# Output projection of a hybrid attention block as seven products of halves, with the gates in another order

## The chip, the cores and the metric

The kernel runs on one core of a Trainium2 chip. A core has a matrix engine (PE; it loads a 128 x 128 block of weights, then multiplies a moving operand into one of eight PSUM banks), a vector engine (DVE), a scalar engine (ACT), a small general engine (POOL) and an engine that only issues transfers (SP). ACT and POOL issue transfers too. All five run their own queues, each in order, and wait for each other through semaphores. The metric is the device time of one execution in microseconds (us); the kernel before takes 1464.66, the median of three runs.

## The reference

One layer over 1024 tokens of 1024 channels, in float32. Two branches work on the same normalised input, gates merge them, and the output projection, to which the change belongs, adds the result to the input:

```python
xn = rmsnorm(x, norm1_g[layer])
u = xn @ w_in[layer].astype(f32)
...
g_a = jax.nn.sigmoid(gate_sb + bg[:D_MODEL])
g_b = jax.nn.sigmoid(gate_hg + bg[D_MODEL:])
merged = g_a * (o_sb @ w_o_sb[layer].astype(f32)) + g_b * (o_hg @ w_o_hg[layer].astype(f32))
h = x.astype(f32) + merged @ w_out[layer].astype(f32)
hn = rmsnorm(h, norm2_g[layer])
a = jnp.square(jax.nn.relu(hn @ w_ff1[layer].astype(f32)))
h = h + a @ w_ff2[layer].astype(f32)
```

`o_sb` is a stick-breaking attention of 8 heads, `o_hg` a gated linear recurrence of 4 heads. A last `rmsnorm` gives the output.

## The kernel before

**Number format.** Each float32 operand of a product is split into a rounded part h (a cast on ACT, `hi_copy`, line 142) and the rest l = x - h (a subtraction on DVE, `lo_sub`, line 147); `hi_lo` does both. `three` (line 490) multiplies h·h, h·l and l·h into one PSUM bank, so a product over 128 channels is three matmuls. The gates and both halves of the MLP are already computed with seven products of halves in place of eight (Winograd's form: sums of operands are multiplied, and the results summed); the output projection is not.

**Stages.** Input norm and transposes; the attention in 64 blocks (8 heads x 8 blocks of queries, `items`), between which pieces of other projections are run; the recurrence; eight gate blocks of 128 channels (`GatePair`, driven by `gates`); the output projection (`wout_job`); the second norm (`norm2_token`) and the transposes of its result (`Quads.fill`, tile hnt, called fills here); the MLP up (`UpPair`) and down.

**Tiles.** SBUF holds 40 large tiles of 1024 columns (`slot`), 10 half ones (`half`), and two each of raw, h and l weight tiles (`wpool`). A tile becomes free when its last reader is done; a transfer that loads into one waits for that. `load` issues on SP's queue, and each load is kept behind the last one.

**Order on PE.** Matmuls belong to one of two lanes, "main" and "fill" (`open_block`); within a lane PE runs them in the order in which the program emits them. On the other engines the order comes from a planner that takes, among the instructions that are ready, the earliest in the program; `after` adds an order by hand.

**Gates.** For channel block cb, `x6`, `y5`, `x7` and `y3` are four products of the gate weights, `hg_product` two of the recurrence's output projection. `late_half` makes the merged activations of tokens 512 to 1023, `early_half` those of tokens 0 to 511. `out` (line 1365) splits the early half into h and l at once, in tiles `mgs`; the late half goes to DRAM (`md`), except for cb 6 and 7, and `late_merged` (line 1375) loads and splits it later.

**Output projection.** `wout_job(n)` covers the columns n x 512 to n x 512 + 511: for each of 8 blocks of 128 tokens, 8 channel blocks x 3 matmuls go into one bank `pw`, which DVE adds to `hres[tb]`, a tile of 128 rows of x (line 1462). `Stream.prefetch` splits the weights ahead. In the second column half each token block is followed by its norm: `norm2_token` squares on ACT, takes a power on POOL, scales on DVE, and stores `hres[tb]` to DRAM from SP (line 1434). From token block 4 on, a fill of two finished token blocks (16 transposes) follows each block, and then the first two MLP pairs begin on half of the tokens.

## Time and profile before

| | |
|---|---|
| runs | 1464.66, 1464.33, 1466.59 us |
| profiled execution | 1464.93 us, of it 1463.1 in the span from the first to the last instruction |
| granted clock of PE | 0.996 of full speed |
| attention | 59.7 to 317.5 us |
| gate blocks | 617.2 to 747.8 us |
| output projection with the first fills | 747.8 to 840.3 us |
| MLP down | 1148.3 to the end |

Times in the profile are us from the span's start, durations of a single instruction ns unless marked. In a row of a group, `out<-in` are the program's tile names without their numbers, `L1462` is a line of the kernel, `x16` the count; then come busy time, mean of one, and the idle time of the engine before them with what ended it. PE busy counts overlapping matmuls once. The durations of matmuls overlap (each is 389 ns long and the next starts earlier), so their cost is read from the spacing in the chain of waits, not from the duration.

### The profile page before, as it was taken

Reading aid. Unit: us, or ns where it says so; the run is one execution under the profiler, and the core shown is the slowest. Engines: PE = TensorE matmul, PEld = TensorE weight load, DVE = VectorE, ACT = ScalarE, POOL = GpSimd, SP = SyncE. Lnnn points to the kernel's source line nnn. Section 1 sums busy time; section 2 is a strip of 40 time slices with the busy share of each in tenths; the row PEclk is TensorE's granted clock in tenths of the full one; section 3 lists DMA queues with packets and bytes.
Section 4 is the critical chain, followed back from the end, with each engine's and each line's share of the span. In section 5 each row is a group of like instructions: output and inputs, shape, how many; then the busy total and the mean of one; then the engine's idle time right before and its main releaser. Section 6 shows DMA issues by size and latency. Waiting matters only on the chain.

```text
span 1463.1 us, 19989 instructions
## 1 busy us (share of the span) xinstructions
PE 1446.2 (99%) x7538; PEld 1231.7 (84%) x7538; DVE 1071.7 (73%) x1545; ACT 655.9 (45%) x1162; POOL 103.5 (7%) x282
## 2 busy tenths in 40 slices
PE   8999999999999999999999999999999999999997
PEld 8889988988898888888888888888888888888885
DVE  6699798798747778877664598666666757768764
ACT  7566666552322334523341574444444533524343
POOL 3020010000000012100000100000000000000041
PEclk9999999999999999999999999999999999999999
DMA  6123022002203249645363133444445974776824
GB/s 205 37 62 73 8 59 65 16 15 62 88 19 101 73 134 252 234 152 159 113 232 108 78 102 129 158 157 148 156 158 185 350 267 175 260 276 249 279 99 161
DMA packets 150248, 206.85 MB, mean 141 GB/s; under 512 B 24668, under 2 KB 92296, under 8 KB 150152
## 3 DMA queue, kind: packets, MB, share of 16 engines
q1 hardware_dynamic: 141464, 182.76, 36.9%
q0 software_dynamic: 5088, 16.26, 4.2%
q10 hardware_dynamic: 3600, 6.56, 1.2%
q8 instruction: 59, 0.97, 0.3%
q14 instruction: 37, 0.30, 0.1%
HBM read 147.35 MB, written 49.81 MB: 135 GB/s over the span
## 4 chain that ended last, share of the span: by engine, by line
PE 91%; DVE 4%; DMA 2%; POOL 1%; issue 1%; ACT 1%; SPq 0%; POOLq 0%; ACTq 0%; DVEq 0%
PE pm L121 18%; PE pX L121 9%; PE pjqk L121 6%; PE pw L121 6%; PE pY L121 6%; PE pW L121 6%; PE pjv L121 3%; PE pjq L121 3%; PE pys L121 3%; PE pyh L121 3%; PE gY L121 3%; PE gX L121 3%; PE pji L121 3%; PE pjf L121 3%; PE pjg L121 3%; PE po L121 3%
## 5 line engine op out<-in xcount | busy, mean ns | idle before, releaser
L142 ACT CAST whid<-w 128x1024 fp32r<-128x1024 f32 x31 | 32.6, 1053 | 153.5 <-PE pm L121 89.2
L679 DVE TENSOR_TENSOR_SCAN rm<-rm,bits 128x511 f32<-128x511 f32 (+7 forms) x72 | 87.3, 1219 | 15.2 <-ACT rm L657 13.5
L121 PE MATMUL pm<-wlod,sh 128*128 128x512 f32 x248 | 96.6, 390 | 0.8 <-DVE wlod L147 0.8
L121 PE MATMUL pm<-whid,sl 128*128 128x512 f32 x248 | 96.5, 389 | 0.0
L121 PE MATMUL pm<-whid,sh 128*128 128x512 f32 x248 | 96.5, 389 | 0.0
L147 DVE TENSOR_TENSOR wlod<-w,whid 128x1024 fp32r<-128x1024 f32 x31 | 37.9, 1222 | 58.1 <-ACT whid L142 58.1
L121 PE MATMUL pm<-th,sh 128*128 128x512 f32 x200 | 77.8, 389 | 0.0
L121 PE MATMUL pm<-tl,sh 128*128 128x512 f32 x200 | 77.8, 389 | 0.0
L121 PE MATMUL pm<-th,sl 128*128 128x512 f32 x200 | 77.8, 389 | 0.0
L147 DVE TENSOR_TENSOR sl<-sa,sh 128x1024 fp32r<-128x1024 f32 x56 | 68.2, 1218 | 0.1
L142 ACT CAST wTh<-pw 128x512 fp32r<-128x512 f32 (+3 forms) x96 | 44.5, 487 | 46.3 <-PE pw L124 39.7
L142 ACT CAST sh<-sa 128x1024 fp32r<-128x1024 f32 x56 | 57.2, 1046 | 10.7 <-DMA sa<-ad 10.7
L147 DVE TENSOR_TENSOR wTl<-pw,wTh 128x512 fp32r<-128x512 f32 (+3 forms) x96 | 50.7, 547 | 9.2 <-ACT wTh L142 5.6
L121 PEld LDWEIGHTS pm<-wlod,sh 128*128 128x128 f32 x248 | 46.6, 188 | 11.0 <-DVE wlod L147 1.2
L121 PEld LDWEIGHTS pm<-whid,sh 128*128 128x128 f32 x248 | 46.5, 188 | 9.7
L121 PEld LDWEIGHTS pm<-whid,sl 128*128 128x128 f32 x248 | 46.5, 188 | 9.6
L155 DVE TENSOR_TENSOR bt<-bt,rm 128x511 f32<-128x511 f32 (+7 forms) x72 | 48.9, 686 | 5.0 <-ACT wf0h L142 0.5
L657 ACT ACTIVATE rm<-z 128x511 f32<-128x511 f32 (+6 forms) x96 | 47.5, 501 | 6.5 <-DVE bt L155 3.3
L121 PE MATMUL pX<-sqh,t1h 128*128 128x512 f32 x128 | 49.9, 390 | 0.0
L121 PE MATMUL pX<-sql,t1h 128*128 128x512 f32 x128 | 49.8, 389 | 0.0
L121 PE MATMUL pX<-sqh,t1l 128*128 128x512 f32 x128 | 49.8, 389 | 0.0
L660 ACT ACTIVATE bt<-z 128x127 f32<-128x127 f32 (+4 forms) x96 | 47.6, 504 | 0.4 <-PE po L121 0.4
(895 smaller groups left out, 4495.3 us busy)
## 6 DMA issues: line engine op xcount, KB each, us to landing
w<-in_w_ff_dram SPq DMA_DIRECT2D x72, 512.0 KB, 4.8
sa<-ad SPq DMA_DIRECT2D x56, 512.0 KB, 7.1
ad<-a SPq DMA_DIRECT2D x32, 256.0 KB, 2.9
ad<-s SPq DMA_DIRECT2D x16, 512.0 KB, 5.6
x<-in_x_dram SPq DMA_DIRECT2D x8, 512.0 KB, 9.6
xnl<-xnh POOLq DMA_DIRECT2D x8, 512.0 KB, 11.3
pr<-pd SPq DMA_DIRECT2D x8, 512.0 KB, 6.1
yr<-yd SPq DMA_DIRECT2D x8, 512.0 KB, 7.7
```

What stands on the lines that cost most here:

```text
L121: return pe(nc.tensor.matmul(*a, **k))
L142: in_turn("act", nc.scalar.copy(dst, src))
L147: nc.vector.tensor_tensor(out=dst, in0=src, in1=hi.bitcast(F32), op=ALU.subtract),
L155: return nc.vector.tensor_tensor(out=out, in0=a, in1=b, op=ALU.mult)
L657: nc.scalar.activation(rm[:, s0 + c0 - 1 : s0 + m - 1], z[:, c0:m], AF.Sigmoid, scale=-0.125)
L660: nc.scalar.activation(bt[:, s0 : s0 + e], z[:, :e], AF.Sigmoid, scale=0.125)
L679: sc = nc.vector.tensor_tensor_scan(out=rr, data0=rr, data1=bits[:, 1024 - nk + a : 1024 - nk + b][:, ::-1], initial=rm[:, b : b + 1] if i ...
```

## The change

The projection is cut into halves of tokens, of channels and of columns, 512 each, and computed by seven products of 512 x 512 x 512.

- The sums of weight blocks that these need (`tw`) are built in DRAM during the attention: four plain copies and four accumulating transfers on POOL's queue, one after every sixth attention block (`out_weight_sums`).
- The sums of merged activations are built on DVE in `out`, and go to DRAM in six forms (`fd`). For that channel blocks cb and cb + 4 must be known together, so `gates` takes the blocks in the order 0, 4, 1, 5, 2, 6, 3, 7. One half form of the last block is split from SBUF, the others are loaded again.
- `out_operands` loads and splits weight forms and merged forms; `out_product` is one block of 128 tokens of one product: 4 channel blocks x 3 matmuls.
- Products in order: 11 (bank W), then 2, 3 and a on top of each other in four banks X, then 1 (Y), b (V) and 4 (Z). `out_start` runs the first four, `out_rest` Y and V, `out_last` Z. After Y the second half of the tokens is finished, so `rows` renames token blocks: `hres[0]` to `hres[3]` are tokens 512 to 1023.
- x is loaded into `hres[4]` to `hres[7]`, and added to `hres[0]` to `hres[3]` by accumulating transfers from POOL once ACT has written W there.
- Norms of token blocks 0 to 3 follow Y, the first two fills stand in V, the norms of 4 to 7 follow Z, with the third fill behind the third Z block. `hres` is stored by POOL in place of SP. The first MLP pair's weights go to large tiles.

```diff
-    md = [dram(f"md{kp}", [P, 2, 512]) for kp in range(KT // 2)]
+    tws = dram("tw", [512, 4, 512])
+    tw = {i: tws[:, i - 1, :] for i in range(1, 5)}
+    fd = {m: [dram(f"fd{m}{kp}", [P, 2, 512]) for kp in range(2)] for m in "1234ab"}
+    def out_block(i, j):
+        return W_OUT[i * 512 : (i + 1) * 512, j * 512 : (j + 1) * 512]
+    def out_weight_sums():
+        b11, b12, b21, b22 = (out_block(i, j) for i in range(2) for j in range(2))
+        for i, src in ((1, b11), (3, b12), (2, b22), (4, b21)):
+            after(nc.gpsimd.dma_start(tw[i], src), lastsel[0])
+            yield
+        for i, src in ((1, b12), (3, b22), (2, tw[1]), (4, tw[2])):
+            after(nc.gpsimd.dma_start(tw[i], src, accum_op=ALU.add), lastsel[0])
+            yield
...
-            if i == 1 and kp < 3:
-                nc.gpsimd.dma_start(md[kp][:, j, :], y)
+            if self.cb < 4:
+                if i == 0:
+                    if j == 0:
+                        mgs.make(0, kp)
+                    hi_lo(*(t[:, j * 512 : (j + 1) * 512] for t in mgs.t[0, kp]), y)
                 return
-            if (i, kp) not in mgs.t:
-                mgs.make(i, kp)
-            h, l = (t[:, j * 512 : (j + 1) * 512] for t in mgs.t[i, kp])
-            hi_lo(h, l, y)
-    def late_merged(kp):
-        r = slot(f"mr{kp}")
-        load(r.rearrange("p (k t) -> p k t", k=2), md[kp])
-        hi_lo(*mgs.make(1, kp), r)
+            def put(m, t):
+                nc.gpsimd.dma_start(fd[m][kp - 2][:, j, :], t)
+            a, b = gp[self.cb - 4].y, self.y
+            a11, a21, a12, a22 = (t[:, c : c + 512] for t in (a, b) for c in (0, 512))
+            if i == 1:
+                s1 = half(f"fs1{self.cb}")
+                sub(s1, a21, a22)
+                put("a", a22)
+                sub(a21, a11, a21)
+                put("3", a21)
+                sub(a11, s1, a11)
+                if self.cb < 7:
+                    put("2", a11)
+                else:
+                    out_operands(m=["2"], last=a11)
+                put("1", s1)
+            else:
+                put("b", a12)
+                s4 = self.p[:, 512:1024]
+                add(s4, a12, a11)
+                put("4", s4)
...
+    gates_in = [gp[4 * i + j] for j in range(4) for i in range(2)]
     def gates():
-        for cb in range(KT):
-            v = gp[cb]
-            n = gp[cb + 1] if cb + 1 < KT else None
+        for v, n, m in zip(gates_in, gates_in[1:] + [None], gates_in[2:] + [None] * 2):
             v.x6()
             v.y5()
             if n:
                 n.split(v.u2_sum)
                 n.load_sums()
-                if cb + 2 < KT:
-                    gp[cb + 2].load()
+                if m:
+                    m.load()
             else:
-                wout_units[0][0].split()
+                out_form["11"].split()
+                out_operands(["2"])
...
-        nc.sync.dma_start(hd[tb], hres[tb])
-    def wout_job(n):
...
+        nc.gpsimd.dma_start(hd[tb], hres[tb])
+    def out_unit(name, src):
+        pieces = [src[i * 256 : (i + 1) * 256, :].rearrange("(k p) c -> p k c", p=P) for i in range(2)]
+        return Unit(f"wout{name}", [[(0, 512, t)] for t in pieces], wide=True)
+    out_form = {"11": out_unit("11", out_block(0, 0))}
+    merged = {}
+    def out_operands(w=(), m=(), last=None):
+        for n in w:
+            src = tw[int(n)] if len(n) == 1 else out_block(int(n[0]) - 1, int(n[1]) - 1)
+            out_form[n] = out_unit(n, src)
+            out_form[n].split()
+        for n in m:
+            merged[n] = []
+            for kp in range(2):
+                r = slot(f"m{n}r{kp}")
+                h, l = slot(f"m{n}h{kp}", F32R), slot(f"m{n}l{kp}", F32R)
+                merged[n].append((h, l))
+                if kp == 0 or last is None:
+                    load(r.rearrange("p (k t) -> p k t", k=2), fd[n][kp])
+                    hi_lo(h, l, r)
+                else:
+                    load(r[:, 0:512], fd[n][kp][:, 0, :])
+                    hi_lo(h[:, 0:512], l[:, 0:512], r[:, 0:512])
+                    hi_lo(h[:, 512:1024], l[:, 512:1024], last)
+    def out_product(ps, a, w, tb, start):
+        open_block("fill")
+        for k in range(4):
+            c = k % 2 * 512
+            sh, sl = (t[:, c + tb * P : c + (tb + 1) * P] for t in merged[a][k // 2])
+            wh, wl = (t[:, c : c + 512] for t in out_form[w].hl[k // 2])
+            three(ps, sh, sl, wh, wl, start and k == 0, k == 3, True)
+    def rows(tb):
+        return slice((tb + 4) % NT * P, ((tb + 4) % NT + 1) * P)
+    left, right = slice(0, 512), slice(512, 1024)
+    oW, oX, oY = {}, {}, {}
+    def turn_dve(ins):
+        in_turn("dve", ins)
+    def out_start():
+        merged["11"] = [mgs.t[0, kp] for kp in range(2)]
+        for tb in range(NT):
+            hres.append(slot(f"h{tb}"))
+        for tb in range(4):
+            load(hres[4 + tb], X[rows(4 + tb), :])
+        out_operands(["3"], ["3"])
+        for tb in range(4):
+            W = bank(f"pwW{tb}")
+            out_product(W, "11", "11", tb, True)
+            nc.scalar.activation(hres[tb][:, right], W, AF.Identity, scale=-1.0)
+            nc.scalar.copy(hres[tb][:, left], W)
+            h = hres[4 + tb]
+            turn_dve(sub(h[:, right], h[:, right], W))
+            turn_dve(add(h[:, left], h[:, left], W))
+            if tb == 1:
+                out_operands(["4"])
+        for tb in range(4):
+            oX[tb] = bank(f"pwX{tb}")
+            out_product(oX[tb], "2", "2", tb, True)
+            h = hres[4 + tb][:, right]
+            turn_dve(sub(h, h, oX[tb]))
+            nc.gpsimd.dma_start(hres[tb], X[rows(tb), :], accum_op=ALU.add)
+            if tb == 0:
+                out_operands(m=["a"])
+            if tb == 2:
+                out_operands(["1"])
+        for tb in range(4):
+            out_product(oX[tb], "3", "3", tb, False)
+            h = hres[tb][:, right]
+            turn_dve(sub(h, h, oX[tb]))
+            if tb == 0:
+                out_operands(m=["1"])
+            if tb == 1:
+                out_operands(["21"])
+            if tb > 1:
+                pairs[tb - 2].load()
+        for tb in range(4):
+            out_product(oX[tb], "a", "4", tb, False)
+            h = hres[tb][:, left]
+            turn_dve(add(h, h, oX[tb]))
+            if tb == 1:
+                out_operands(m=["b"])
+            if tb == 2:
+                out_operands(["22"])
+            if tb > 1:
+                pairs[tb - 2].split()
+    def out_rest(tb):
+        if tb < 4:
+            oY[tb] = bank(f"pwY{tb}")
+            out_product(oY[tb], "1", "1", tb, True)
+            for h in (hres[tb][:, right], hres[4 + tb][:, right]):
+                turn_dve(add(h, h, oY[tb]))
+        else:
+            W = bank(f"pwV{tb}")
+            out_product(W, "b", "21", tb - 4, True)
+            h = hres[tb][:, left]
+            turn_dve(add(h, h, W))
+    def out_last(tb):
+        Z = bank(f"pwZ{tb}")
+        out_product(Z, "4", "22", tb, True)
+        h = hres[4 + tb][:, right]
+        turn_dve(add(h, h, Z))
...
-                if self.j in (1, 2):
+                if self.j < 3:
...
-            q.dma_start(OUT[tb * P : (tb + 1) * P, cs], y[:, cs])
+            q.dma_start(OUT[rows(tb), cs], y[:, cs])
...
+    wsums = out_weight_sums()
...
             scores(*items[i + 2])
+        if i % 6 == 5:
+            next(wsums, None)
...
-    gp[1].load()
+    gates_in[1].load()
     gates()
...
-    st2.finish(j_wout - 2)
-    st2.advance(7, j_wout - 1)
-    first[0].load()
-    first[0].split()
-    first[0].sums()
-    st2.finish(j_wout - 1)
-    first[1].load()
+    out_start()
     g2b[0] = slot("g2b")
     load(g2b[0], norm2_g[0].partition_broadcast(P))
-    for tb in range(NT):
-        st2.advance(1, j_wout)
-        if tb == 1:
-            first[1].split()
-            first[1].sums()
+    sides = {}
+    for tb in range(4):
+        out_rest(tb)
+        sides[tb] = norm2_token(tb)
+        next(sides[tb])
+        if tb > 0:
+            next(sides[tb - 1], None)
+    for tb in range(4):
+        out_rest(4 + tb)
+        if tb == 0:
+            next(sides[3], None)
+        if tb < 2:
+            first[tb].sums()
+        if tb == 0:
+            out_operands(m=["4"])
+        if tb > 1:
+            hn.fill(tb - 2, hsrc, "hn")
+        if tb == 3:
+            hn.sums(0, 1)
+    for tb in range(4, NT):
+        out_last(tb - 4)
         if tb == NT - 1:
             for u in first:
                 last_evac[0] = after(u.sum_hi(1), last_evac[0])
@@ -1946,20 +2068,16 @@
         next(side)
         if tb == NT - 1:
             hn.sums(2, 1, then=False)
-        if tb in (4, 5, 6):
-            hn.fill(tb - 4, hsrc, "hn")
-        if tb == 5:
-            hn.sums(0, 1)
+        if tb == 6:
+            hn.fill(2, hsrc, "hn")
         for _ in side:
             pass
-        if tb == 6:
-            hn.sums(1, 1)
-    st2.finish(j_wout)
     pairs[2].load()
     first[1].w1(0, 256)
     first[0].w2(0, 256)
     first[0].sum_lo(1)
     first[1].w2(0, 256, range(2))
+    hn.sums(1, 1)
     hn.fill(3, hsrc, "hn")
     first[1].w2(0, 256, range(2, 4))
     for u in first:
```

More of the change, by code (lines that the diff above doesn't have):

```diff
@@ L1401 @@
     hres = []
-    st2 = Stream(eager=True)
-    wout_units = []
     hn = Quads()
@@ L1433, in norm2_token @@
         hd[tb] = dram(f"hd{tb}", [P, D])
-        nc.sync.dma_start(hd[tb], hres[tb])
-    def wout_job(n):
-        cs = slice(n * 512, (n + 1) * 512)
-        units = [
-            Unit(
-                f"wout{n}{i}",
-                [[(0, 512, W_OUT[i * 256 : (i + 1) * 256, cs].rearrange("(k p) c -> p k c", p=P))]],
-                wide=True,
-            )
-            for i in range(4)
-        ]
-        wout_units.append(units)
-        def body():
-            for tb in range(NT):
-                if n == 0:
-                    if tb < 3:
-                        late_merged(tb)
-                    hres.append(slot(f"h{tb}"))
-                    load(hres[tb], X[tb * P : (tb + 1) * P, :])
-                    if tb in AHEAD_AT:
-                        st2.prefetch()
-                ps = bank(f"pw{n}_{tb}")
-                for kt in range(KT):
-                    sh, sl = mgs.stat(kt, tb)
-                    wh, wl = (w[:, kt % 2 * 512 : (kt % 2 + 1) * 512] for w in units[kt // 2].hl[0])
-                    three(ps, sh, sl, wh, wl, kt == 0, kt == KT - 1)
-                nc.vector.tensor_tensor(
-                    out=hres[tb][:, cs], in0=hres[tb][:, cs], in1=ps, op=ALU.add
-                )
-                yield
-        return st2.add(units, body)
@@ L1469 @@
-    AHEAD_AT = (2, 4, 6)
-    for n in range(2):
-        j_wout = wout_job(n)
+        nc.gpsimd.dma_start(hd[tb], hres[tb])
[22 more added lines that the diff above has]
+                    hi_lo(h[:, 512:1024], l[:, 512:1024], last)
```

1 line of the change is left out of this document (removed).

## The prediction

> **What bounds the kernel now.** I read first the busy shares of the page, then the chain of waits that ended last, then a table of windows by stage.
>
> ```profile
> span 1463.1 us, 19989 instructions
> PE 1446.2 (99%) x7538; PEld 1231.7 (84%) x7538; DVE 1071.7 (73%) x1545; ACT 655.9 (45%) x1162; POOL 103.5 (7%) x282
> ...
> 747.95 70.72 PE pw L121 x312
> 818.67 1.75 PE hnt L124 x16
> 820.41 5.46 PE pw L121 x24
> 825.88 1.75 PE hnt L124 x16
> 827.62 5.46 PE pw L121 x24
> 833.08 1.75 PE hnt L124 x16
> 834.83 5.46 PE pw L121 x24
> ...
> 846.18 1.75 PE hnt L124 x14
> 847.93 6.47 PE pW L121 x54
> 854.40 5.47 PE pX L121 x24
> ```
>
> Columns of the chain are start, length, what. PE is the bound, and in the output projection (pw, 312 + 3 x 24 = 384 matmuls) it is the whole chain: 70.72 / 312 = 0.2267 us a matmul, 24 for one block of 128 tokens in 5.44 us. Four bursts of 16 transposes (hnt, the "fills", 1.75 us each) stand between and behind the blocks. So a matmul removed here is time removed, as long as nothing else becomes late. What could is in the windows (us; then busy time of PE, PEld, DVE, ACT, POOL with instruction counts, clock, DMA share, GB/s):
>
> ```profile
> 617.20:747.80 130.60, 130.60 (x578) 108.12 (x577) 93.05 (x132) 43.56 (x59) 3.37 (x7) 1.00 0.45 145
> 747.80:834.80 87.00, 87.00 (x410) 72.78 (x409) 41.72 (x57) 26.65 (x53) 4.48 (x12) 1.00 0.41 151
> 834.80:870.00 35.20, 34.55 (x207) 30.66 (x206) 32.57 (x55) 25.33 (x49) 2.72 (x5) 1.00 0.33 105
> 747.80:893.00 145.20, 144.55 (x716) 122.50 (x715) 94.99 (x140) 65.67 (x122) 7.20 (x17) 1.00 0.37 132
> 59.70:317.50 257.80, 256.54 (x1625) 229.18 (x1623) 227.64 (x324) 166.22 (x383) 28.69 (x152) 1.00 0.17 42
> ```
>
> The gates (617.2 to 747.8) and the projection up to its last block (834.8) have PE without a gap and DVE at 71% and 48%. From 834.8 on, where the MLP is entered, DVE is at 32.57 / 35.20 = 92.5%, and there PE has its only gap, 0.65 us. The last line is the attention.
>
> **The change part by part.**
>
> **1. Fewer matmuls.** Seven products of 512 x 512 x 512 are 7 x 4 token blocks x 4 k x 3 = 336 matmuls in place of 384, of the same shape. 48 x 0.2267 = **-10.9 us**. One block of one product takes 12 x 0.2267 = 2.72 us, the whole stage 76.2 us in place of 87.0. Nothing here is uncertain but a slower matmul, for which there is no reason.
>
> **2. Weight sums in the attention.** Eight transfers of 1 MB, DRAM to DRAM, four of them accumulating, go on POOL's queue, one every sixth of 64 blocks. Blocks take (317.2 - 59.9) / 64 = 4.0 us, so one every 24 us:
>
> ```profile
> L124 PE MATMUL pw<-ident,bt x288: 270/272/300, 59.9 to 317.2; 128*128 128x128 f32 x144
> ...
> L1175 POOL DMA_DIRECT2D xnl<-xnh x8 | 7.2, 944 | 29.4 <-PE pjg L121 26.9 <-PE pgq L121 2.4
> ...
> DMA to landing us min/median/max: 4.7/11.3/15.3
> L590 POOL DMA_DIRECT2D QH<-QH x16 | 8.7, 544 | 106.5 <-ACT QH L142 85.0 <-ACT wTh L142 12.8 <-DVE bt L155 8.7
> ```
>
> The nearest row is the accumulating xnl<-xnh: 512 KB, 0.94 us of POOL, 4.7 to 15.3 us to land. POOL is busy 28.69 of 257.8 us and the DMA share is 0.17, so both have room: 8 x 0.94 = 8 us of POOL, hidden by its idle time. Behind a transfer on POOL stand the memsets of bt and wT and the copies of QH and QL; score blocks run two blocks, some 8 us, ahead. The last sum (tw4 += tw2) must wait on POOL for tw2 += tw1 issued 24 us before. At twice the longest row, 30.6 us, POOL stands 6.6 us, still under the 8. Value 0; bounds 0 and +4 (if half of that lead is gone). The Trainium skill, page "DMA: Bandwidth & Descriptors", section "Anatomy of one DMA — SWDGE (gpsimd) path", prices such a transfer at about 2.0 us plus bytes over 436 GB/s, an estimate of 4.4 us for 1 MB. By it POOL never waits and the sum is the same 0; the trace does not bear it out for accumulating ones, 11.3 us median where it gives 3.2.
>
> **3. Gates in pairs (0, 4, 1, 5, ...).** The products and the loads of each block are the same; only their order changes, so SP's queue gets as many. Blocks 4 to 7 lose one split (a cast and a subtract of 512 columns) and gain three subtracts and an add; the two late splits of 6 and 7 go as well. POOL gets 24 stores for 6.
>
> ```profile
> L147 DVE TENSOR_TENSOR msl<-yr,msh 128x512 fp32r<-128x512 f32 x10 | 6.9, 693 | 6.4 <-ACT msh L142 6.3
> L1368 POOL DMA_DIRECT2D md<-yr x6 | 3.2, 540 | 92.1 <-DVE yr L1072 92.1
> ```
>
> DVE: (16 - 6) x 0.69 = +6.9 us into 130.6 - 93.05 = 37.6 us of idle; POOL 18 x 0.54 = 9.7 us into an idle engine. Operands of a block are made one block (16.3 us) ahead, which hides it: 0, and +6.9 if that cover were gone. The first product needs only blocks 0 to 3, done 16 us earlier; block 7's last half, which the projection waited closely for, is now needed last.
>
> **4. Loads of the projection.** Sixteen product blocks (the first 43.5 us) come with four loads of x (128 rows each), five weight forms, four merged forms, two pairs of MLP weights and four accumulations of x: about 15 MB.
>
> ```profile
> 748.00:760.00 12.00, 12.00 (x54) 9.95 (x53) 7.56 (x10) 5.25 (x7) 0.00 (x0) 1.00 1.00 372
> ```
>
> At the 372 GB/s of this full window that is 42 us. But only 10 MB (28 us) are needed inside the 43.5 us; the forms of the last two products and the MLP weights have 10 to 30 us more. The x accumulations (512 KB each) can start when ACT has written W, at about 4, 7, 10 and 12 us, and are needed from 24 us on by a DVE sum, by PE (whose fourth product waits for that sum) from 33 to 41. Two at a time, as the xnl rows ran, they land by 30 us: 0. One after another at 11.3 us the fourth lands at 49: +8. I take 0: the rows overlapped. SP issues its loads in order and each waits for free tiles: of the 40 large tiles I count 36 to 40 in use through these 43.5 us, so a form is loaded about one product (10.9 us) ahead and no more.
>
> **5. DVE's load.** The projection's sums:
>
> ```profile
> L1462 DVE TENSOR_TENSOR h<-h,pw 128x512 f32<-128x512 f32 x16 | 11.0, 686 | 22.5 <-PE pw L121 22.3 <-DMA h<-in_x_dram 0.2
> L147 DVE TENSOR_TENSOR msl<-mr,msh 128x1024 fp32r<-128x1024 f32 x3 | 3.7, 1226 | 2.5 <-ACT msh L142 2.5
> L142 ACT CAST msh<-mr 128x1024 fp32r<-128x1024 f32 x3 | 3.2, 1053 | 4.8 <-DMA mr<-md 4.8
> ```
>
> Sums of h: W 8, the three X 4 each, Y 8, V 4, Z 4, in all 36 for 16: 20 x 0.69 = +13.7. Splits of 1024 columns behind 747.8: five weight and five merged forms of two pieces and one form's two, 22, for 4 + 3 = 7: 15 x 1.23 = +18.4. Two short splits less: -1.4. That is +30.7, so from 747.8 to 893 DVE needs 125.7 us in 145.2 - 10.9 = 134.3: **93.6%**, against 65% before. ACT gets 15 x 1.05 and 8 copies of W, 21 us, and stays at 65%. At the best share that a stretch with this work shows (19.11 of 20.00 us, below) 125.7 us fit in 131.5: no loss. At the 92.5% of 834.8 to 870 they take 135.9: 1.6 us too long. At the 86% of the stage before the gates (66.45 of 77.00) 146: 11.9.
>
> ```profile
> 540.00:617.00 77.00, 76.84 (x425) 64.30 (x424) 66.45 (x98) 34.71 (x65) 16.35 (x23) 1.00 0.74 220
> 850.00:870.00 20.00, 20.00 (x107) 17.29 (x106) 19.11 (x24) 14.81 (x20) 0.00 (x0) 1.00 0.23 73
> ```
>
> Much of it is made ahead, but what is late at the end is paid in full: the first form for the MLP (sql below) is finished as pX starts at 854.40. I take **+2.0**, bounds 0 and +12.
>
> ```profile
> 852.95 2.36 DVE L147 TENSOR_TENSOR sql<-hnq,sqh 128x1024 fp32r<-128x1024 f32 x2 [0.79 <-ACT sqh L142]
> ```
>
> **6. The norm's chain against shorter blocks.** A token block's way from its last matmul to its transposes is sum, square, power, scaling:
>
> ```profile
> 818.71 0.69 DVE L1462 TENSOR_TENSOR h<-h,pw 128x512 f32<-128x512 f32 x1 [1.34 <-PE pw L121]
> 819.49 1.06 ACT L1418 ACTIVATE hn<-h 128x1024 f32<-128x1024 f32 x1 [4.35 <-DVE h L1462]
> 821.00 0.55 POOL L233 TENSOR_TENSOR n_y<-n_ss,expo 128x1 f32<-128x1 f32 x1
> 821.59 1.28 DVE L1429 SCALAR_TENSOR_TENSOR hn<-h,n_y,g2b 128x1024 f32<-128x1024 f32 x1 [2.19 <-POOL n_y L233]
> ```
>
> It ends at 822.87, 4.2 us after the block did (818.67). Blocks took 5.44 us, so it was covered. In the new order the third fill, which takes blocks 4 and 5, is emitted right behind the third Z block, 2.72 us after block 5's own; PE keeps that order, so it stands 4.2 - 2.72 = **+1.5** (bounds 0 and +3, when DVE is busy with the first two fills' splits). The fourth fill's gap, 0.65 us now, follows one Z block closer on the third; ACT has that fill's copies, two casts of 1.1 us and the last squares to do in between: **+0.4**, bounds -0.65 and +2. The stores of h move from SP to POOL: 8 x 0.54 us there, issued as soon as the sum is done, while the square runs: 0, up to 0.5.
>
> **Sum:** -10.9 + 1.5 + 2.0 + 0.4 = -7.0. The profiled execution took 1464.93 us around its span of 1463.1, 0.3 above the median of 1464.66. 1464.93 - 7.0 = 1457.9; from the median 1457.7. I say **1458**.
>
> **The rivals.**
>
> **All hidden (1454 to 1455.5).** Terms 5 and 6 vanish: 1464.7 - 10.9 = 1453.8. For it: 48% DVE use before 834.8. Against it: the order of block 5 and the third fill is fixed, so about 1 us stays.
>
> **DVE eats most of it (1461 to 1467).** DVE waits for loads that land late and keeps 87 to 90% where 93.6 are wanted: 125.7 / 0.89 = 141.2, 6.9 us over, and the 1.5 of term 6 with it: 1453.8 + 8.4 = 1462. For it: in the gates, with the same kinds of operations, it idles 29%, on ACT and PE. Against it: those idle stretches were not under load.
>
> **DVE becomes the bound (slower, about 1470).** It is one queue in order; a split whose load is late holds up the sums behind it, PE then waits for a free bank. This decides from a share of 125.7 / 145.2 = 86.6%: below that the stage is longer than before. At 83%, between the 86% before the gates and their 71%, it takes 151.4, 6.2 us more than 145.2: 1470.9. Against it: it needs idle time in a queue whose work is mostly ready 10 us ahead.
>
> **The sums by transfer stop the attention.** If an accumulation of 1 MB takes over 24 + 8 = 32 us, POOL holds the memsets and PE stands for what is over. To be worse than no change it must take over 39; the row scales to 30.6 at most.
>
> **How the numbers follow.** A measurement here can tell about 0.2% (2.9 us) from no change: faster is below 1461.7, slower above 1467.6. Chances: forecast (1455.5 to 1461) 0.52, all hidden 0.14, DVE eats most 0.20 (a quarter of it still under 1461.7), DVE bound 0.11, attention stopped 0.03. Faster 0.71, same 0.15, slower 0.14. The range goes from all hidden, 1454, through the second rival to 1467; outside are the two slow cases and a little at the low end.
>
> **What would show it.** Right: 336 matmuls between the gates and the first MLP product, a gap of 1 to 3 us before the third fill's block 5 transposes (released by DVE hn), DVE above 90% from the projection to the MLP's first pairs, attention and gates as long as before. Wrong: PE gaps in the attention with POOL as releaser (part 2); gaps before products released by a load or a split (4, 5); PE waiting in the MLP's entry for sql by more than 3 us; or no gap at the third fill.

## The result and the profile after

The changed kernel takes 1470.49 us (median of 6 runs, 1469.50 to 1471.36), the kernel before 1464.87 beside it: a ratio of 1.0036, 95% interval 1.0026 to 1.0046. It is 5.6 us slower where 7 us less were forecast, and above the range. From the page of the changed kernel:

```profile
span 1469.2 us, 20065 instructions
...
PE 1441.4 (98%) x7490; PEld 1227.8 (84%) x7490; DVE 1105.7 (75%) x1591; ACT 671.9 (46%) x1180; POOL 132.0 (9%) x319
...
q0 software_dynamic: 11376, 35.40, 9.3%
```

PE has its 48 matmuls less (7490 for 7538) and less busy time, yet the span grew by 6.1 us. The table of windows says where (columns as in the prediction); first three stretches of the attention, the gates, the projection up to the first MLP product pX, three parts of it, and a longer stretch that step 5 of the prediction speaks of:

```profile
240.00:250.00 10.00, 10.00 (x50) 8.30 (x49) 7.79 (x11) 4.20 (x8) 1.58 (x4) 1.00 0.74 119
250.00:260.00 10.00, 4.86 (x22) 4.29 (x21) 5.72 (x9) 5.43 (x12) 0.38 (x3) 0.76 0.51 143
260.00:270.00 10.00, 10.00 (x65) 9.21 (x65) 9.04 (x13) 5.65 (x12) 0.45 (x5) 0.90 0.19 55
624.30:754.90 130.60, 130.60 (x578) 108.16 (x577) 101.19 (x144) 42.79 (x56) 11.14 (x22) 1.00 0.58 194
754.90:862.60 107.70, 99.02 (x498) 83.50 (x497) 84.24 (x129) 57.31 (x109) 22.43 (x32) 0.97 0.63 204
754.90:809.50 54.60, 54.60 (x242) 45.26 (x241) 40.35 (x52) 29.43 (x37) 6.46 (x10) 1.00 0.94 298
809.50:834.60 25.10, 22.32 (x112) 17.93 (x111) 25.07 (x40) 11.22 (x31) 7.43 (x10) 1.00 0.16 61
840.00:845.00 5.00, 4.65 (x18) 4.36 (x19) 2.62 (x5) 3.93 (x13) 1.60 (x3) 0.50 0.69 220
754.90:901.20 146.30, 137.62 (x668) 115.47 (x667) 120.45 (x174) 82.33 (x142) 22.43 (x32) 0.98 0.51 170
```

The same two stages of the kernel before:

```profile
240.00:250.00 10.00, 10.00 (x50) 8.31 (x49) 8.86 (x12) 6.33 (x12) 0.38 (x3) 1.00 0.35 105
250.00:260.00 10.00, 10.00 (x67) 8.85 (x65) 9.79 (x15) 7.48 (x18) 0.83 (x8) 1.00 0.19 55
...
747.80:854.40 106.60, 105.95 (x546) 90.55 (x545) 58.74 (x95) 40.55 (x89) 7.20 (x17) 1.00 0.41 148
```

- **Attention: +7.1 us.** The gates start at 624.3 for 617.2 and are as long as before (130.60).
- **Projection: +1.1 us** in place of -10.9. PE idles 107.70 - 99.02 = 8.7 us (0.65 before), and its matmuls, which should need 105.95 - 10.9 = 95.05 us, are 4.0 us slower at a granted clock of 0.97.
- MLP up: -0.1 us. MLP down: -2.0, nearly all of it behind the last matmul, where the result is stored. This stage takes 312.4 to 314.3 us in the profiled executions of the changed kernel and its variants, and 315.0 and 316.2 in the two that keep the old projection (the kernel before and e8 below). Whether these 2 us are a gain of the change no run tests.

**The gap in the attention.** The timeline of ACT, after (start, length, what; in brackets the idle time before it and what ended it):

```profile
243.75 0.50 ACT L142 CAST wTh<-pw 128x384 fp32r<-128x384 f32 x1
253.09 1.04 ACT L142 CAST wg0h<-wg0r 128x1024 fp32r<-128x1024 f32 x1 [8.85 <-DMA wg0r<-in_w_in_dram]
254.05 0.58 ACT L142 CAST wTh<-pw 128x512 fp32r<-128x512 f32 x1
```

and before:

```profile
247.78 1.05 ACT L142 CAST wg0h<-wg0r 128x1024 fp32r<-128x1024 f32 x1 [3.62 <-DMA wg0r<-in_w_in_dram]
248.73 0.58 ACT L142 CAST wTh<-pw 128x512 fp32r<-128x512 f32 x1
```

SP issues the load wg0r at 244 us in both. It lands after 3.9 us before and 9.1 after, and the cast that waits for it stands in ACT's queue ahead of wTh, a piece of the attention. POOL's timeline shows what was in flight, the eighth weight sum, issued 3 us earlier, and the waits of PE show what it cost:

```profile
240.74 1.20 POOL L1100 DMA_DIRECT2D tw<-tw  x1
```

```profile
PE po L121 <- DVE wTl L147: 5.1, 1, 5.1
```

5.1 us of idle PE, and behind it a granted clock of 0.76 and 0.90 (the windows above), which makes up the other 2. Earlier sums slowed loads too: the two of wi0r (206 to 224 us) landed after 6.8 us (median) in place of 3.6. PE waited for neither: their casts stand in ACT's queue only at 240.3 and 242.8 us.

**The projection.** The chain of waits, after:

```profile
798.58 10.89 PE pwY L121 x48
...
818.51 4.87 DVE hn L1462 x4
...
828.04 2.68 DVE sql L147 x8
830.73 0.67 DVE sq L347 x2
...
833.41 0.61 DVE h L1072
...
834.31 0.60 POOL hd L1467
...
837.06 1.28 POOL n_ss L230
...
839.01 1.30 DVE hn L1462
840.35 3.25 PE hnt L124 x14
843.60 3.78 PE pwZ L121 x12
...
850.51 2.12 POOL n_ss L1458
...
852.72 0.20 POOL n_ss L230
...
854.39 1.75 PE hnt L124 x14
```

Up to 809.5 us PE runs through. From there the chain belongs to DVE, busy for 25.07 of the next 25.10 us (windows). The sum of h with the first Z block, whose matmuls end at 830.2, begins only at 833.3, behind eight sums of quarters (sq, hnq) that nobody needs yet. The third fill then waits 2.62 and 1.50 us; 14 transposes take 3.25 us for 1.75, and 12 matmuls 3.78 for 2.72, since the clock is down (0.50 from 840 to 845). POOL's store of h and a slow n_ss stand in the chain too. So two things had to be told apart: which transfer does the harm in the attention, and whether DVE, POOL's stores or the norm's chain make the projection late.

### The profile page after: what moved, and what is told of

Its sections match the earlier page's. It is cut to its first block, busy times and chain, and to the rows that moved or that the text cites. A ratio compares the mean times of both kernels' runs of the same rounds, so it can differ in the third digit from the quotient of the medians.

```text
span 1469.2 us, 20065 instructions
## 1 busy us (share of the span) xinstructions
PE 1441.4 (98%) x7490; PEld 1227.8 (84%) x7490; DVE 1105.7 (75%) x1591; ACT 671.9 (46%) x1180; POOL 132.0 (9%) x319
## 4 chain that ended last, share of the span: by engine, by line
PE 89%; DVE 5%; DMA 2%; POOL 1%; issue 1%; ACT 1%; SPq 0%; POOLq 0%; ACTq 0%; DVEq 0%
PE pm L121 18%; PE pX L121 9%; PE pjqk L121 6%; PE pY L121 6%; PE pW L121 6%; PE pjv L121 3%; PE pys L121 3%; PE gY L121 3%; PE gX L121 3%; PE pyh L121 3%; PE pji L121 3%; PE pjg L121 3%; PE pjf L121 3%; PE po L121 3%; PE pjq L121 2%; PE z L121 2%
## 5 line engine op out<-in xcount | busy, mean ns | idle before, releaser
L142 ACT CAST sh<-sa 128x1024 fp32r<-128x1024 f32 x56 | 57.2, 1046 | 10.9 <-DMA sa<-ad 10.9
L1809 POOL TENSOR_SCALAR fss<-fss 128x1 f32<-128x1 f32 x8 | 4.5, 561 | 563.0 <-ACT fsc L1804 562.5
```

Source lines behind the costliest of these rows:

```text
L142: in_turn("act", nc.scalar.copy(dst, src))
L1809: nc.gpsimd.tensor_scalar(out=ssq, in0=ssq, scalar1=1.0 / D, scalar2=EPS, op0=ALU.mult, op1=ALU.add)
```

## The experiments

Times are medians; the kernel before took 1464.5 to 1465.5 beside them. "Stage" is the time from the first product to the first pX (107.6 after, 106.5 before; 95.6 is that of before less 10.9, the measure for a change without loss). It is read in the one profiled execution of each run, whose time lies up to 2.7 us from the median (e7: 1465.07), so it is rougher than the medians.

| run | us | ratio to before, 95% | stage |
|---|---|---|---|
| e1_every_fifth | 1463.83 | 0.9990 (0.9981 to 0.9999) | 106.7 |
| e2_without_last | 1465.12 | 1.0002 (0.9992 to 1.0011) | 107.5 |
| e8_before_and_sums | 1472.02 | 1.0047 (1.0035 to 1.0060) | 106.5 |
| e3_h_store_sp | 1470.05 | 1.0039 (1.0026 to 1.0051) | 107.5 |
| e4_fill_behind | 1469.40 | 1.0036 (1.0024 to 1.0049) | 106.5 |
| e5_z_order | 1467.45 | 1.0017 (1.0008 to 1.0026) | 104.6 |
| e6_z_order_weights | 1468.80 | 1.0027 (1.0017 to 1.0038) | 104.8 |
| e7_all_three | 1462.38 | 0.9985 (0.9976 to 0.9994) | 105.9 |
| e9_z_order_fifth | 1461.18 | 0.9975 (0.9966 to 0.9985) | 104.5 |
| e10_no_differences | 1459.14 | 0.9960 (0.9947 to 0.9972) | 102.0 |
| e11_stores_behind | 1461.15 | 0.9974 (0.9965 to 0.9983) | 104.3 |
| e12_combined | 1464.18 | 0.9995 (0.9986 to 1.0004) | 107.1 |
| e13_constant_scale | 1460.45 | 0.9964 (0.9951 to 0.9978) | 104.7 |
| e14_constant_no_differences | 1458.58 | 0.9952 (0.9940 to 0.9965) | 100.9 |
| e15_differences_pool | 1464.79 | 0.9998 (0.9990 to 1.0007) | 108.7 |
| e16_scale_on_act | 1462.32 | 0.9979 (0.9970 to 0.9988) | 105.2 |

### The attention: e1, e2, e8

```diff
-        if i % 6 == 5:
+        if i % 5 == 4:
             next(wsums, None)
```

> The changed kernel with its eight weight-sum transfers after every fifth attention block in place of every sixth, so that the last one is issued near 210 us and not at 240.74 us, 3 us ahead of the load wg0r. Theory A (the last accumulation slows that load, which landed after 9.1 us in place of 3.9, and its cast holds ACT's queue): wg0r lands in 3.5 to 5 us, no PE gap at 250 us, gates start at 617 to 618 instead of 624.3, time 1463 to 1464.5. Rival B (the extra memory traffic of the attention as a whole costs 7 us, wherever it stands): gap of the same size somewhere from 180 to 260 us, time 1469 to 1472. Rival C (the accumulation hits another load at its new place, wi0r at 207 to 224 us): PE gap of 2 to 7 us there, time 1466 to 1472.

e2 ends the loop of accumulations at `(2, tw[1])`. e8 puts `out_weight_sums` and its call, as changed, into the kernel before.

> The changed kernel without the eighth transfer (tw4 += tw2); the weight form 4 is then incomplete, and everything else is issued as before. Theory A (that one transfer beside the load wg0r is the whole loss of the attention): gates start at 617 to 618 instead of 624.3, granted clock 1.00 from 250 to 270 us, time 1463 to 1464.5. Rival B (all transfers together): 1/8 of the 7 us comes back, time 1469.5 to 1470.5. Rival D (the gates or the planner's order of the attention moved, not the transfers): no change, 1470 to 1471.

> The kernel before with nothing added but the eight weight-sum transfers in its attention, whose result it doesn't use. Theory A (the eighth, issued 3 us ahead of the load wg0r, holds ACT's queue by that load): PE gap of 4 to 5.5 us near 250 us, granted clock below 1 behind it, gates start near 624 instead of 617.2, time 1470.5 to 1472. Rival D (the loss of the attention comes from other parts of the change, say the planner's other order): no gap, 1464 to 1465.5.

Windows of e1 and of e8:

```profile
250.00:260.00 10.00, 10.00 (x67) 8.87 (x65) 9.79 (x14) 7.49 (x19) 0.83 (x8) 1.00 0.18 55
```

```profile
250.00:260.00 10.00, 4.87 (x24) 4.38 (x23) 5.72 (x9) 5.45 (x12) 0.38 (x3) 0.83 0.53 148
```

Theory A holds three times. With the last sum at 215.0 us the load lands in 3.6 us, the gates start at 616.3, and the kernel gains 6.7 us. Without the last sum they start at 617.1, with a gain of 5.4, a little less than expected. Added to the kernel before, the sums alone cost 7.2 us, with the same gap at the same place. The other seven sums cost nothing that can be seen.

### The projection, first round: e3 and e4

```diff
-        nc.gpsimd.dma_start(hd[tb], hres[tb])
+        nc.sync.dma_start(hd[tb], hres[tb])
```

> The changed kernel with the stores of h issued by SP again, as in the kernel before, and no longer by POOL. Theory E (the stores stand in POOL's queue ahead of and between the norms' small operations, so powers of blocks 0 to 3 came at 811 to 818 us though the squares were done at 805 to 811): powers within 3 us of the squares, the gap ahead of the first fill (0.59 + 0.76) gone, that ahead of the third (2.62 + 1.50) down to about 2.5, projection 107.7 us down to 103 to 105.5, time 1466 to 1468.5. Rival F (DVE, 99.8% busy from 809.5 to 826, is what is late): powers earlier but the scalings no sooner, time 1469.5 to 1471. Rival G: SP holds a store until h is finished, and the loads behind it (form 4 of the merged activations) land late: a gap ahead of the first Z product, time 1470 to 1475.

Nothing is won (1470.05). ACT's timeline in e3:

```profile
808.79 1.05 ACT L142 CAST mbh<-mbr 128x1024 fp32r<-128x1024 f32 x1 [10.73 <-DMA mbr<-fdb]
...
813.85 1.05 ACT L1451 ACTIVATE hn<-h 128x1024 f32<-128x1024 f32 x1
```

SP held two stores until h was finished, the load of mbr behind them came late, and the squares stood behind its cast: rival G, at another load than expected. The stores had only changed queues, so e3 didn't decide between E and F.

e4 takes `hn.fill(2, hsrc, "hn")` from behind the third Z block to behind `first[0].w1(0, 256)`.

> The changed kernel with the third fill behind the last Z block and the first half MLP product (2.72 + 2.9 us of matmuls) and no longer ahead of them. Theory H (the gaps ahead of the third fill, 2.62 + 1.50 us, are a norm chain of two token blocks that had no cover, and the slow matmuls behind them, about 2.5 us, are the clock after the gap): the gap goes down to 0 to 1, matmuls at 0.227 us spacing, gap ahead of the fourth fill up by 0.5 to 2, time 1464.5 to 1468. Rival I (DVE and ACT are short and the same time is lost later): a gap of 4 us or more ahead of the fourth fill or of the MLP's products, time 1469 to 1472.

The gap ahead of the third fill is gone, and the same time is lost later. PE's waits in e4:

```profile
PE pW L121 <- ACT p L1679: 4.0, 2, 3.2
```

The copy of p stands in ACT's queue behind squares that wait for DVE: rival I, in the main (1.1 us gained).

### DVE's order: e5, e6, e7, e9

e5 holds the sums of quarters behind the third fill, and the scaling of block tb behind the next Z block's sum:

```diff
-            nc.vector.scalar_tensor_tensor(
+            scaled[tb] = nc.vector.scalar_tensor_tensor(
...
+            after(scaled[tb], z_add.get(tb - 3))
...
-        if tb == 3:
-            hn.sums(0, 1)
...
         if tb == 6:
             hn.fill(2, hsrc, "hn")
+            hn.sums(0, 1)
```

> The changed kernel with one part of DVE's order in the Z stage changed: the eight sums of the first two fills' quarters (hnq, sq; 3.0 us from 830.64 on) stand behind the third fill and no longer ahead of the sums of h with the first two Z blocks; the scaling of block 4 stays behind the second of these, that of block 5 behind the third. Nothing else moves. Theory F (DVE, without a pause from 809.5 to 834.6 us, makes the norms late: what stands ahead of the sums of h decides): sums of Z0 and Z1 about 3 us sooner, gap ahead of the third fill from 2.62 + 1.50 to about 1.5 in all, slow matmuls behind it gone, projection 107.7 down to 103.5 to 105.5, time 1466 to 1468.5. Theory E (POOL's stores of h make them late): chain of block 5 as long as before behind its sum, gain under 1 us, 1469.5 to 1470.5. Rival J: the eight sums are missed later, ahead of the fourth fill or the MLP's products: 1469 to 1472.

e6 adds `first[0].sums(scaled[3])` and `first[1].sums(scaled[5])`, which hold the weight differences behind those scalings. e7 is e6 with every fifth block, e9 is e5 with every fifth block.

> The same order in the Z stage, and besides the eight differences of MLP weights (0.69 us each, w_0r and w_1r) held behind the scaling of block 3 and of block 5; in the changed kernel six of them stand on DVE between 809.5 and 818.5 us. Theory F: mbl 0.7 us sooner for V1, first fill without its waits of 0.59 + 0.76, so 1.5 to 2.5 us less than with the Z order alone: 1464 to 1467. Theory E: powers still come at 813 to 818 us, so the scalings and the first fill stay: same time as the Z order alone, within 0.7 us. Rival J: the late weight forms (t1h, t1l) are waited for in the MLP's entry: 1 to 3 us slower than the Z order alone.

> The kernel of the two orders on DVE together with the weight-sum transfers after every fifth attention block. If the two losses are independent, its time is that of the two orders less 6 to 7 us: 1457.5 to 1461, below the kernel before (1464.5) and near the forecast 1458. If the gap in the attention and the losses in the projection shared a cause (say, a longer clock or memory effect), the gains overlap and it stays above 1462.

> The kernel with the Z order (1467.45) and the weight-sum transfers after every fifth attention block (which alone gave 1463.83 for 1470.49). If the two losses are independent: 1467.45 - 6.6 = 1460.9, so 1460 to 1462, faster than the kernel before. If they share a cause: above 1463.

e5 gains 3.0 us by order alone, as theory F expected; DVE's timeline has the sum of the first Z block at 829.61 for 833.32, 2.7 us sooner when counted from the stage's start. e6 takes away most of the first fill's waits (0.23 for 1.35 us), but is 1.35 us slower than e5, near the lower end of rival J. The third fill waits 2.3 us for 1.8 and the fourth 2.5 for 2.3, so the order has moved waits and not only removed them. In all, PE still waits 1.1 us less than in e5 (5.7 for 6.8); what is lost again in the profiled execution is 1.3 us of PE's busy time (99.06 for 97.78), slower matmuls behind the gaps. In e9 the two gains add up as expected (1461.2 for 1460.9): with the weight sums moved and the Z order the changed kernel beats the kernel before, by 3.7 us. In its profiled execution 2.0 us of that are the stage (104.5 for 106.5) and another 2 the end of the MLP down, whose cause is open. e7 (1462.38) lies outside the 1457.5 to 1461 expected for two independent losses, but that range was counted from the expected e6; from the measured one it is 6.4 us less, so the gains add up there too, and e6's loss stays.

### Load, stores or the length of the chain: e10 to e16

All start from e9. e10 omits `first[tb].sums()`; e11 issues the stores of h by `after(nc.gpsimd.dma_start(hd[tb], hres[tb]), last_pow[0])` behind later powers; e13 scales by `expo[:, 0:1]` in place of `r`; e14 is both e10 and e13.

> As the Z order with every fifth block, but without the eight differences of the first two MLP pairs' weights (w_0r and w_1r, 0.69 us each on DVE, 5.5 us in all); four of their seven products then multiply the plain weight blocks. Theory F (DVE has too much to do between the last Y block and the first MLP product): projection 2.5 to 5.5 us shorter (104.5 us down to 99 to 102), first fill without a wait, time 1456 to 1458.5. Rival K (what is left is the length of the norm's chain and the clock behind the gaps, and DVE's load is nothing): first fill sooner by 1 to 1.4, all other gaps as before, 1459 to 1461.

> As the Z order with every fifth block, but POOL issues the stores of h of blocks 0 to 3 behind the power of block 3, of 4 and 5 behind the power of 5, of 6 and 7 behind the power of 7, so that none stands ahead of a norm it could delay. Theory E (the stores on POOL make the norms late): powers of blocks 0 to 3 at 803 to 810 us on this kernel's clock of events rather than 806 to 813, gaps ahead of the third and fourth fill down by 0.6 to 1.2 each, 1458.5 to 1460. Theory F (DVE): within 0.7 us of the same kernel without this edit, and the small POOL operations still run up to 1 to 2 us long beside DVE's.

> As the Z order with every fifth block (1461.2; 104.5 us of projection), but the scaling of each token block takes a constant (-0.5) in place of the norm's power, so that it follows the sum of h at once; squares and powers still run, their results unused. DVE's work is the same. Theory L (length of the norm's chain): gaps ahead of the third (0.6 + 1.76) and the fourth fill (0.4 + 2.26) and the slow clock behind them gone, 4 to 6 us: 1455 to 1457.5. Theory F (DVE's load): the scalings still stand behind DVE's queue; first fill's 1.35 and mbl's 1.3 stay, and 1 to 2 us at most are won: 1459 to 1460.5.

> As the kernel with the constant scale, and besides without the eight differences of MLP weights (5.5 us of DVE; alone worth 2.0 us of time and 2.5 of projection). If load and chain are separate terms, the gains add: 2 us below the run with the constant alone. If the chain was the one cause and the differences only stood in its way at the first fill: 1.3 to 1.5 us below. If DVE's load was the one cause: both together leave under 1 us of PE gaps, and the projection comes to 96.5 to 98 us.

The stages of e9, e10, e13 and e14, in this order, and PE's waits in e13:

```profile
747.98:852.46 104.48, 97.69 (x497) 82.69 (x496) 84.57 (x129) 58.26 (x109) 21.23 (x32) 0.98 0.64 211
```

```profile
746.97:848.96 101.99, 95.94 (x498) 81.33 (x496) 79.86 (x121) 58.03 (x109) 21.19 (x32) 1.00 0.65 216
```

```profile
747.38:852.08 104.70, 97.92 (x497) 82.75 (x496) 85.30 (x130) 58.90 (x109) 29.31 (x32) 0.98 0.64 211
```

```profile
746.94:847.87 100.93, 95.99 (x497) 81.34 (x496) 80.06 (x121) 58.28 (x109) 29.29 (x32) 1.00 0.66 218
```

```profile
PE hnt L124 <- DVE hn L1463: 3.1, 3, 1.8
PE pW L121 <- DVE sql L147: 2.2, 1, 2.2
PE pwV L121 <- DVE mbl L147: 1.3, 1, 1.3
```

The stores behind the powers don't change the time (1461.15 for 1461.18). The first power does come sooner, 7.0 us in the stage (POOL starts it at 799.05, 49.6 us into it, for 804.60, 56.6 into it), but the four scalings that take the powers begin at the same point, 63.6 us into it, behind DVE's other work. DVE's timeline in e9 and in e11:

```profile
811.59 4.87 DVE L1463 SCALAR_TENSOR_TENSOR hn<-h,n_y,g2b 128x1024 f32<-128x1024 f32 x4
```

```profile
813.00 4.86 DVE L1465 SCALAR_TENSOR_TENSOR hn<-h,n_y,g2b 128x1024 f32<-128x1024 f32 x4
```

The first fill waits the same 1.35 us. The fourth waits 1.11 for 2.26, but the next product then waits 2.24 for sql. So theory E falls.

The constant scale (e13) cuts square and power out of the chain and gains 0.7 us (1.2 measured against the kernel before beside each), which the intervals of e9 and e13 can't tell from nothing. The fourth fill no longer waits, but the next product waits 2.2 us for sql: DVE is late with whatever comes next. For the third fill e13 is no test of theory L. Its wait of 1.76 us is the same in e5, e9, e10, e11, e13 and e14, since e5's order holds the scaling of block 5 behind the sum of h with the third Z block, whether the power is needed or not. DVE's timeline in e14 shows it idle ahead of that sum, and the scaling right behind it, though the h of block 5 was ready at 823.6:

```profile
825.62 0.69 DVE L1072 TENSOR_TENSOR h<-h,pwZ 128x512 f32<-128x512 f32 x1 [0.84 <-PE pwZ L121]
826.22 2.65 DVE L1463 SCALAR_TENSOR_TENSOR hn<-h,expo,g2b 128x1024 f32<-128x1024 f32 x2
```

In e9 the power of block 5 is done at 829.1 and its scaling begins at 829.6, so there the order costs 0.5 us at most; in e13 and e14 it hides what the constant scale would have saved. So theory L is not borne out at the first fill and the fourth, and stays open at the third.

5.5 us of work taken from DVE (e10) gain 2.0 us, and 1.9 on top of the constant scale (e14): two separate terms that add, as e14's first case has it. The intervals overlap, so the sizes are uncertain. Less work on DVE helps, as F has it, but not by F's size. e10's 1459.14 lies in rival K's range and not in F's, and as K said the gaps ahead of the third and the fourth fill are unchanged (1.76 and 2.26). Of the 2.5 us by which e10's stage is shorter only 0.7 are waits of PE (6.8 down to 6.05); the rest is busy time, 95.94 us for 97.69, because in this execution the clock stayed up behind the same gap (last section). That was luck of the execution, and it was in e14 too (95.99 for 97.92). DVE's load as the one cause would have left under 1 us of gaps in e14; there are 4.9, and a stage of 100.9 us, 5.3 above the measure. The waits are 2.2 us for sql, 1.8 at the third fill, 0.7 for mbl and 0.2 at the first fill; no run took them away.

e12 puts all orders together, e15 runs the differences on POOL, e16 the scalings of blocks 0 to 3 on ACT (`nc.scalar.mul(hsrc[tb][:, cs], hres[tb][:, cs], r)`), with the norm's weights in the copies out of the fills' banks.

> All edits of order together: weight sums after every fifth block, Z order, stores of h behind the powers, the eight differences behind the scaling of block 3, and the sum of h with the last Z block ahead of the sums of quarters. Theory F with E as a small part: first fill without its 1.3 us, fourth fill's gap 2.26 + 0.4 down to under 1.5, and with it the slow matmuls behind it: 1456.5 to 1459.5. Rival J (what is put off is missed as late weight or activation forms in the MLP's entry): 1460 to 1463.

> As the Z order with every fifth block, with the eight differences on POOL, behind the power of block 3, where POOL is idle for some 16 us. Nothing is left out. If POOL runs them at 1 to 1.5 us each and doesn't hold DVE: as without the differences, 1459 to 1460. If the two engines hold each other up (POOL's small operations took 0.19 us alone and 1.0 to 2.3 beside DVE's): the differences take 2 us and more each, block 4's norm waits on POOL's queue, 1461.5 to 1466.

> As the Z order with every fifth block (1461.2; projection 104.5), with the scalings of token blocks 0 to 3 (4.87 us of DVE in a row) on ACT, and the norm's weights of these blocks applied by ACT's copies out of the transposes' banks, 32 of 128 columns in place of 16 of 256. Nothing is left out. Theory F (DVE's load): first fill's waits gone, m4l and the sums of h with V and Z sooner, projection 101.5 to 103, time 1458.5 to 1460. Rival M (ACT, idle for 8 us ahead of the first fill and 4 behind the second, becomes late by its longer copies, and sql with it): waits ahead of the first MLP products, 1461 to 1464.

None is faster than e9. In e12 the differences stand ahead of the sums of Z0 and Z1, and the third fill waits 2.62 and 1.25 us again. e15's groups on POOL and DVE, 800 to 830 us (busy, mean ns):

```profile
L1640 POOL TENSOR_TENSOR w_1r<-w_1r,w_1r 128x512 f32<-128x512 f32 x2 | 4.5, 2262 | 0.0
```

```profile
L1465 DVE SCALAR_TENSOR_TENSOR hn<-h,n_y,g2b 128x1024 f32<-128x1024 f32 x4 | 6.9, 1793 | 0.0
L147 DVE TENSOR_TENSOR sql<-hnq,sqh 128x256 fp32r<-128x256 f32 x8 | 6.0, 824 | 0.0
```

The same eight subtractions sql take 2.8 us in e9 and 6.0 here, while POOL works: load put on POOL comes back to DVE. In e16 the first two fills don't wait at all, but ACT's 32 short copies take 1.0 us of the first Z product, and the fills behind wait for 5.6 us together: rival M.

## Why the prediction was wrong, step by step

- **1, fewer matmuls: right.** 336 matmuls run, the first 240 of them without a gap up to 809.5 us, at 0.2267 us each.
- **2, weight sums: this step failed.** It gave 0 with bounds of 0 and +4; it cost 7.1. It priced the transfers' time on POOL and who waits behind them there, and its rival, POOL holding the memsets, didn't happen: POOL ran the memsets of that block at 240.27, ahead of the transfer. The last two sums landed after 11.2 us (median), well inside the 30.6 allowed for; their length was not the fault. What was missing: who else loads at that moment (wg0r on SP), who waits at the head of ACT's queue for that load, and that PE's clock falls after such a gap. The mean DMA share of 0.17 over the attention hid it; in the 10 us that count it rose from 0.35 to 0.74. The lead of two score blocks, 8 us, helped nothing, since wT stood behind the cast.
- **3, gates: right.** 130.60 us both; DVE +8.1 us for the +6.9 expected, all of it behind PE.
- **4, loads: right for PE.** It waited for no load, and the x accumulations were hidden, though they were issued 11.8 to 16.6 us into the stage and not at 4 to 12. DVE did wait 7.4 us in the first half, behind casts of late forms (m3r, wout1r).
- **5, DVE's load: the mechanism was right, the size was not.** The work came near its estimate (120.45 us from 754.9 to the matching end, 901.2, for 125.7). But the term spread it over 134 us, at a share of 93.6%: +2.0. The share was 82% over this stretch, 74% up to 809.5 and 99.9% from there to 834.6. In the first half of the stage DVE idled 14.25 of 54.6 us, which work whose operands came later could not use, and from 809.5 to 834.6 it had no pause; what was needed there was late at once (by order alone 3.0 us of it came back in e5, by less work 2.0 in e10). The bound of +12 held, the choice within it didn't.
- **6, the norm's chain: mis-sized.** Third fill +1.5, measured 4.12 and the slow matmuls behind it; fourth fill 1.05 expected, 1.79 measured; at the first fill 1.35 where nothing was expected. The chain of 4.2 us was counted from the block's last matmul, with DVE free; it began when DVE came to the first Z block's sum, 3.1 us late. The gap of 1.50 ahead of block 5's transposes is the forecast's own number, but by luck: block 5's matmuls ended at 832.9 and its transposes began at 840.35, so its chain took 7.4 us and not 4.2; PE spent the rest in the wait of 2.62 for block 4. The stores of h at 0 to 0.5 were right (e11: 0.0).
- Steps 5 and 6 together were forecast at 3.9 and cost 12.0 (8.0 of PE's idle time, 4.0 of slow matmuls). **The rivals:** "DVE eats most of it" (1461 to 1467) gives the time without the loss of the attention (e1: 1463.83). Its mechanism, DVE waiting for late loads, shows in 7.4 of the 14.25 us of idle time, but no run tested what they cost. "DVE becomes the bound" names the slow side, but by itself it didn't get there; the total came from step 2. "The sums stop the attention" was right in place and sign, wrong in its mechanism and its point of decision.

## What to carry to other kernels

A transfer that is free on its own queue is priced at the loads it runs beside: look up which load is issued within its landing time, and what stands behind that load's consumer in an engine's order. An engine's load is to be summed over the stretch in which its operands exist, not over the stage. Where it is at 100% there, one order gained 3.0 us here (e5), further ones moved the loss elsewhere (e6, e11, e12, e16), and less work gained 2.0 (e10). Issuing the last of eight transfers some 25 us sooner was worth 6.7 us here, nearly as much as the whole change was forecast to bring.

## What the runs showed of the hardware

**The clock after a gap.** In e5 a gap of 2.26 us ahead of the fourth fill was followed by 14 transposes in 3.25 us and a granted clock of 0.78:

```profile
850.00:855.00 5.00, 5.00 (x36) 5.00 (x35) 4.88 (x16) 3.70 (x12) 0.00 (x0) 0.78 0.00 0
```

In e10, with the same 2.26 us at the same place, they took 1.75, and the clock stayed at 1.00:

```profile
841.00:846.00 5.00, 3.90 (x33) 3.69 (x32) 5.00 (x16) 3.14 (x12) 0.00 (x0) 1.00 0.00 0
```

So a gap of this length may or may not cost 1.5 us more. The Trainium skill, page "TensorE: Matmul & The Clock Gate", section "Part 1: The HAM clock gate", lets the clock fall after at least one idle window of about 3.4 us, and calls the window free-running. That the same gap falls out both ways fits a free window; the length doesn't, since 2.26 us were enough here.

**POOL beside DVE.** The operation n_ss of line 230 on one column takes 0.20 us or 1.28 (chain above), its sum of two halves 2.11 when DVE runs without a pause; it ends as DVE's long subtraction does (852.6):

```profile
850.51 2.11 POOL L1458 TENSOR_TENSOR n_ss<-n_ss,n_ss 128x1 f32<-128x1 f32 x1 [1.52 <-ACT hn L1451]
```

```profile
851.36 1.22 DVE L147 TENSOR_TENSOR t1l<-w_0r,t1h 128x1024 fp32r<-128x1024 f32 x1
```

The Trainium skill, page "SBUF — State Buffer", section "SBUF: two separate sides", says that the two engines share a pair of ports, which one instruction holds to its end while the other waits; of DVE's instructions only those with two inputs in SBUF (as this subtraction has) or in a two-port mode take part. e15 agrees. The rows above fit in the common end (852.62 and 852.58), but n_ss is recorded from 0.85 us before this subtraction, so they don't show that a single instruction held it up.
